# The first half of a convolution turned before the value projection, its first taps beside the indexer's chunks

## Chip, core and metric

One core of a Trainium2 chip runs the whole program in one launch. The metric is the device time of that launch in microseconds (us), the median of several executions.

## What is computed

Two layers; in each, three token mixers read the same normalised input, and one large input projection (`proj = h @ w_in`) feeds them all. Sequence 256, model width 2048, float32. Branch B holds what is moved here: a gated pair of projections, then a causal depthwise convolution of 31 taps over 1024 channels.

```
def conformer_conv(u, conv_w, conv_b, ln_w, ln_b):
    a, gt = jnp.split(u, 2, axis=-1)
    y = a * jax.nn.sigmoid(gt)
    y = lax.conv_general_dilated(y, conv_w..., window_strides=(1,), padding=[(CONV_WIDTH - 1, 0)],
                                 feature_group_count=CONV_CH) + conv_b
    y = layer_norm(y, ln_w, ln_b)
    return jax.nn.silu(y)
...
    y_a = (dsa_attention(qa, ka, va, qi, ki, wi, top_k) * jax.nn.silu(za)) @ w_a_out
    y_b = (conformer_conv(ub, ...) * jax.nn.silu(zb)) @ w_b_out
    y_c = (stick_breaking_attention(qc, kc, vc) * jax.nn.silu(zc)) @ w_c_out
    merged = g[:, :, 0] * y_a + g[:, :, 1] * y_b + g[:, :, 2] * y_c
    return x + merged @ w_out
```

## The kernel before

Every matmul multiplies float32 by splitting each operand into a high part and a low part, with three products of the parts. The weights stream from memory in units of 128x1024 numbers (512 KB). A unit goes through three engines. SyncE loads it into `raw` (five buffers). ScalarE (ACT) casts it into `wh` (L255, `high`), VectorE (DVE) subtracts into `wl` (L259, `low`), and TensorE (PE) multiplies with both. `wh` and `wl` have three buffers each, so ACT and DVE may work at most about three units ahead of PE.

The parts of a layer that matter here run in this order on PE: the opening (first half of the convolution's two gated projections, result in the two tiles `sgs`), `values(0)` (8 units, 12 matmuls of 512 columns each), `index_chunk(0)` and `index_chunk(4)` (8 units each; a unit has 6 matmuls of 512 columns and 8 of 192), then "U's group" (`run(gather(...))` with the key steps, the seven products of `Seven` for the second half of the gated projections, and the rest of that half), then `index_chunk(8)` and `(12)`. In the text, "unit 8" is the first of `index_chunk(0)`, counted from the first of `values(0)` as 0; units 8 to 23 are the two chunks, and the first key step follows them.

`turned(srcs, use)` transposes a result through memory: two STREAM_TRANSPOSE on DVE (L299), four DMAs on the POOL queue out to `z` (L302), one DMA back into `zy` (L308), and then `use`. The argument `later` says how many units after the issue `use` is placed. `use_u` copies `zy` into `yT` on ACT (L1062) and starts the taps. A tap of the convolution is done in one of two ways, chosen by the string `pace[0]` at every unit: "2" lets DVE multiply and add for two of the four channel blocks (L731), "s" lets ACT make the four products (`products_of`, L726) into a buffer, and DVE adds the buffer to the sum at a later unit (`added`, L1032). With "s" the buffer is the tile `one`, a single one; with "1" and the like it is one of two. `hold[0]` keeps the taps from being issued at all. The engines execute in the order written; Tile's scheduler writes it, so a change of the Python code moves instructions on all engines.

Of the kernel before, what the change touches and what calls it, by code (L numbers as in the profile page):

```python
# [30 lines left out]
LATER = 10  # L31
# [20 lines left out]
def trunk(ctx: ExitStack, tc: tile.TileContext, x, w_in, xt, w_a, w_b, w_c, w_out,  # L52
# [16 lines left out]
    def issue_after(ins):  # L69
        return nullcontext() if fixed[0] else tc.issue_after(ins)  # L70
# [29 lines left out]
    def nm(s):  # L100
        uid[0] += 1
        return f"{s}_{uid[0]}"
# [44 lines left out]
    def ev():  # L147
        return tp.tile([P, 512], F32, tag="ev", bufs=3, name=nm("ev"))
# [4 lines left out]
    waiting = []  # L153
# [11 lines left out]
    @contextmanager  # L165
    def in_turn():
        with tc.high_priority(offset=URGENT), issue_after(newest_parts[1].ins):
            yield
# [18 lines left out]
    def background(mm):  # L187
        while pending and pending[0][0] <= count[0]:
            step_on(pending[0])
        for e in stages[:2]:  # L190
            if e[1] <= count[0]:
                with issue_after(mm.ins), tc.high_priority() if urgent[0] else nullcontext():
                    advance(e)
                break
# [8 lines left out]
    hold, calls, pace, urgent = [False], [0], ["2"], [False]  # L203
# [59 lines left out]
    def unit(*args, **kw):  # L263
        u = load_unit(*args, **kw)
        high(u)
        low(u)
        return u[1:]
# [23 lines left out]
    def away(srcs, tmp, soon=False):  # L291

        n = len(srcs)
        k = srcs[0].shape[1]
        tmp = tmp.rearrange("p (t b k i) -> p t b k i", b=4, k=k, i=32)
        z = dp.tile([n, 4, 32, 4, k * 32], F32, tag=f"z{k}", bufs=4, name=nm("z"))
        with nullcontext() if soon else tc.high_priority():
            for t, src in enumerate(srcs):
                nc.vector.transpose(tmp[:, t].rearrange("p b k i -> p k b i"),  # L299
                                    src.rearrange("p k (b c) -> p k b c", b=4, c=32))  # L300
            for a in range(4):
                nc.gpsimd.dma_start(z[:, :, :, a, :].rearrange("t b c e -> c (t b) e"),  # L302
                                    tmp[a * 32:(a + 1) * 32].rearrange("c t b k i -> c (t b) (k i)"))
        return z

    def back(z, y):

        nc.gpsimd.dma_start(y.rearrange("p (t a) k i -> p t (a k i)", a=4), z.rearrange("t b c a e -> (b c) t (a e)"))  # L308

    def turned(srcs, use, later=LATER, tmp=None, soon=False):  # L310


        n = len(srcs)
        if tmp is None:
            tmp = tp.tile([P, n * 512], F32, tag="zt", bufs=1, name=nm("zt"))
        c = srcs[0].shape[1]
        z = away([v.rearrange("p (k e) -> p k e", e=P) for v in srcs], tmp[:, :n * c], soon)

        def rest():
            y = tp.tile([P, n * 512], F32, tag="zy", bufs=1, name=nm("zy"))  # L320
            y = y[:, :n * c].rearrange("p (u k i) -> p u k i", u=n * 4, i=32)
            back(z, y)
            yield later - 2
            yield from use(y)

        pending.append([count[0] + 2, rest()])
# [49 lines left out]
    def token_accs():  # L376
        return [acc_tile() for _ in range(NT)]
# [10 lines left out]
    def chunk_N(w, segs, act, nk, ku=2, accs=None, ks=None):  # L388
        n = sum(c for _, c in segs)
        if accs is None:  # L390
            accs = token_accs()
        for k0 in range(*(ks or (0, nk)), ku):
            background(token_products(accs, n, unit(w, k0, ku, segs), act, k0, ku, nk, range(NT)))
        return accs
# [326 lines left out]
    def products_of(yT, pr, j, q, dst, bias=False):  # L721
        for c in range(j * 4, j * 4 + 4):
            wq = pr[:, P_CW + c * TAPS + q:P_CW + c * TAPS + q + 1]
            b = dict(bias=pr[:, P_CB + c:P_CB + c + 1]) if bias else {}
            v = dst[:, c % 4 // 2, c % 2 * S:(c % 2 + 1) * S]
            nc.scalar.activation(v, yT[:, c, q:q + S], AF.Identity if bias else AF.Copy, scale=wq, **b)  # L726

    def tap(yT, cv, pr, c, q):
        wq = pr[:, P_CW + c * TAPS + q:P_CW + c * TAPS + q + 1]
        o = cv[:, c, :]  # L730
        nc.vector.scalar_tensor_tensor(o, yT[:, c, q:q + S], wq, o, op0=ALU.mult, op1=ALU.add)  # L731
# [35 lines left out]
    for layer in range(DEPTH):  # L767
# [9 lines left out]
        with tc.manual_schedule(engines={nc.vector.engine}), ExitStack() as order:  # L777
# [27 lines left out]
            sgs = [ev() for _ in range(2)]  # L805
# [217 lines left out]
        def taps(j, yT=yT, cv=cv, pr=pr, one=one, two=two, halves=halves):  # L1023

            o = cv[:, j * 4:j * 4 + 4, :]
            o2 = o.rearrange("p (t c) f -> p t (c f)", t=NT)
            state = dict(q=1, c=0, sum=None)

            def added():
                if state["sum"] is None:  # L1030
                    return False
                nc.vector.tensor_add(o2, o2, state["sum"])  # L1032
                state["sum"] = None
                return True

            halves.append(added)

            def begin():
                products_of(yT, pr, j, 0, o2, True)

            def go():
                by = pace[0][calls[0]]
                if added() and by == "s":
                    by = ""
                q = state["q"]
                if q < TAPS and by:
                    if state["c"] or by == "2":
                        for c in range(2):
                            tap(yT, cv, pr, j * 4 + state["c"] + c, q)
                        state["c"] = (state["c"] + 2) % 4  # L1050
                    else:
                        state["sum"] = one if by == "s" else two[:, q % 2]
                        products_of(yT, pr, j, q, state["sum"])
                    state["q"] += not state["c"]
                if state["q"] < TAPS or state["sum"] is not None:
                    waiting.insert(0, [0, [go]])

            waiting.append([4, [begin]])
            waiting.append([1, [go]])

        def use_u(j, y, yT=yT):
# [57 lines left out]
        def index_unit(acc, low_, k0, w_):  # L1119
            wh, wl = w_  # L1120
            for k in range(2):
                kk = k0 + k
                for i in range(2):
                    mult(acc[0], part(hx, i, kk, 1, slice(P, S))[:, 0, :], wh[:, k, :], kk + i == 0,
                         kk == KD - 1 and i == 1)
                mult(acc[1], hq[:, kk, :], wh[:, k, :], kk == 0, kk == KD - 1)
            for k in range(2):
                kk = k0 + k
                for f in range(4):
                    mm = mult(low_[:, f, :], wl[:, k, f * P:(f + 1) * P], hi(hx, kk)[:, 0, TOPK:],  # L1130
                              kk == 0 and f % 2 == 0, kk == KD - 1)
            return mm

        def low_tile():
            return mm_tile().rearrange("p (f t) -> p f t", f=4)[:, :, :S - TOPK]

        def index_done(h, acc, low_):
            e = t4()[:, :4 * (S - TOPK)].rearrange("p (k t) -> p k t", k=4)
            with tc.high_priority():
                nc.scalar.copy(e, low_)  # L1140
            turned(acc, partial(use_i, h, e), LATER + 1 if h < NIH - 4 else LATER - 2)
# [31 lines left out]
        def index_chunk(h):  # L1173
            acc, low_ = token_accs(), low_tile()
            for k0 in range(0, KD, 2):
                if (h, k0) in between:
                    between[h, k0]()
                background(index_unit(acc, low_, k0, unit(w, k0, 2, [(O_QI + h * P, 512)])))
            index_done(h, acc, low_)
# [8 lines left out]
        def values(j):  # L1188
            a = chunk_N(w, [(O_VC + j * 512, 512)], hx, KD, accs=None if j else wide_accs())
            if j:  # L1190
                with in_turn():
                    for f in halves:
                        f()
            for t in range(NT):
                with tc.high_priority():
                    nc.scalar.copy(vcr[:, t, j * 512:(j + 1) * 512], a[t])

        values(0)
        index_chunk(0)
        index_chunk(4)  # L1200
        def turn_first():
            with in_turn():
                turned(sgs, partial(use_u, 0))

        keys = key_steps()
        keys[7].at(0, turn_first)
        ring[0], spare[0] = 0, 10 ** 9
        run(gather("y*2 g.M1a y g.M5a g.M1b y g.M5b y g.M6a y g.M6b y g.M2a y g.M2b g.M7a g.M7b g.M3a c g.M3b c g.M4a d g.M4b c d c d d",
                   g=u, y=keys, c=ug, d=ua))
# [495 lines left out]
        begin = "g.M1a y g.M5a g.M1b y g.M5b y g.M6a y g.M6b y g.M2a y g.M2b y g.M7a y g.M7b "  # L1705
# [156 lines left out]
```

## Time and profile before

| | us |
|---|---|
| median of 3 runs | 1982.86 (1982.69 to 1982.94) |
| the profiled execution, its own time | 1982.91 |
| its span, first to last instruction | 1981.1 |
| PE busy | 1970.6 |
| DVE busy | 1724.0 |
| ACT busy | 1302.1 |

The share of busy time of each engine stands in the page's first section. A timeline row of the profile reads: start, duration, engine, source line, operation, tile written and tiles read, size, how many merged, and in square brackets how long the engine was idle before and what ended that. In a row of windows the brackets (x) count instructions. The lines of the source in the rows are those of the kernel before; after the change lines behind 1198 have numbers smaller by two.

### The profile page before, as it was taken

To read this page: it belongs to the slowest core of one execution; us is meant where nothing else is said; L and a number is where in the kernel's file an instruction comes from. 1 tells how busy PE (TensorE), PEld (TensorE's weight loads), DVE (VectorE), ACT (ScalarE), POOL (GpSimd) and SP (SyncE) were. 2 spreads that over 40 slices of the span, in tenths; PEclk is the share of its full clock that TensorE was granted. 3 is DMA by queue.
4 is the path that set the end of the run, shared out by engine and by line. 5 is a ranking of instruction groups with operands and counts; after the bars stand their busy time and mean duration, and the time that the engine had idled before them with its cause. 6 is when DMAs were issued, how large, how long until landed. Compare 5 with 4: busy or idle time off the path is not lost. (4 is left out here: it accounts for less than half of the span.)

```text
span 1981.1 us, 26165 instructions
## 1 busy us (share of the span) xinstructions
PE 1970.6 (99%) x9194; PEld 1648.1 (83%) x9194; DVE 1724.0 (87%) x2054; ACT 1302.1 (66%) x1668; POOL 215.0 (11%) x320
## 2 busy tenths in 40 slices
PE   9999999999999999999999999999999999999998
PEld 8888888888888888888888888888888888888886
DVE  8798999989988979878786989999888888798786
ACT  7567666579875666564565666565898766565654
POOL 0021111200200001011100210121001000010010
PEclk9999999999999999999999999999999999999999
DMA  8888768876878778787978887688669688787894
GB/s 277 278 262 261 239 180 262 257 223 188 260 239 264 212 228 271 243 273 271 321 232 277 252 264 224 192 259 273 200 188 279 213 276 250 217 276 235 288 287 137
DMA packets 247557, 486.90 MB, mean 246 GB/s; under 512 B 17984, under 2 KB 30784, under 8 KB 247296
## 3 DMA queue, kind: packets, MB, share of 16 engines
q1 hardware_dynamic: 217472, 406.03, 63.2%
q0 software_dynamic: 28288, 76.04, 14.6%
q10 hardware_dynamic: 1664, 3.15, 0.4%
q8 instruction: 72, 1.18, 0.2%
q14 instruction: 61, 0.50, 0.1%
HBM read 452.38 MB, written 32.77 MB: 245 GB/s over the span
## 5 line engine op out<-in xcount | busy, mean ns | idle before, releaser
L270 PE MATMUL acc<-wh,s 128*128 128x512 f32 x4096 | 1039.8, 390 | 0.0
L255 ACT CAST wh<-raw 128x1024 fp32r<-128x1024 f32 (+1 forms) x639 | 666.9, 1046 | 416.6 <-PE acc L270 271.2
L259 DVE TENSOR_TENSOR wl<-raw,wh 128x1024 fp32r<-128x1024 f32 (+1 forms) x640 | 773.3, 1213 | 154.7 <-ACT wh L255 147.0
L270 PEld LDWEIGHTS acc<-wh,s 128*128 128x128 f32 x4096 | 761.4, 188 | 153.2 <-DVE acc L579 0.5
L270 PE MATMUL acc<-wl,s 128*128 128x512 f32 x1856 | 517.0, 390 | 0.0
L270 PEld LDWEIGHTS acc<-wl,s 128*128 128x128 f32 x1856 | 346.0, 188 | 74.8 <-DVE wl L259 4.4
L270 PE MATMUL mm<-wh,s 128*128 128x512 f32 (+1 forms) x1376 | 335.2, 385 | 0.0
L270 PEld LDWEIGHTS mm<-wh,s 128*128 128x128 f32 x1376 | 257.3, 188 | 50.9 <-ACT ev L1688 0.5
L302 POOL DMA_DIRECT2D z<-zt x192 | 113.2, 612 | 795.6 <-DVE zt L299 743.4
L270 PE MATMUL mm<-wl,s 128*128 128x512 f32 (+1 forms) x688 | 180.9, 385 | 0.0
L255 ACT CAST wh<-ar 128x1024 fp32r<-128x1024 f32 x92 | 96.9, 1053 | 81.0 <-PE acc L270 33.6
L270 PEld LDWEIGHTS mm<-wl,s 128*128 128x128 f32 x688 | 128.7, 188 | 24.4
L259 DVE TENSOR_TENSOR wl<-ar,wh 128x1024 fp32r<-128x1024 f32 x92 | 112.1, 1220 | 21.1 <-ACT wh L255 21.1
L731 DVE SCALAR_TENSOR_TENSOR s<-yT,cst,s 128x256 f32<-128x256 f32 x216 | 94.5, 476 | 0.1
L726 ACT ACTIVATE ar<-yT,cst 128x256 f32<-128x256 f32 x192 | 83.7, 499 | 15.4 <-DVE t L1330 12.6
L255 ACT CAST wh<-va 128x1024 fp32r<-128x1024 f32 x55 | 57.7, 1050 | 44.8 <-PE acc L270 19.5
L259 DVE TENSOR_TENSOR wl<-va,wh 128x1024 fp32r<-128x1024 f32 x55 | 67.1, 1219 | 20.6 <-ACT wh L255 20.6
L528 POOL DMA_DIRECT2D ar<-in_w_in_dram x28 | 33.8, 1220 | 453.0 <-DVE wl L259 453.0
L270 PEld LDWEIGHTS mm<-s,wl 128*128 128x128 f32 x512 | 66.9, 191 | 5.0
L308 POOL DMA_DIRECT2D zy<-z x50 | 36.1, 722 | 293.2 <-DMA z<-zt 75.8
L270 PE MATMUL mm<-s,wl 128*128 128x192 f32 x512 | 66.0, 271 | 0.0
L726 ACT ACTIVATE s<-yT,cst 128x256 f32<-128x256 f32 x88 | 40.4, 517 | 38.3 <-DVE s L1032 38.1
(284 smaller groups left out, 1463.3 us busy)
## 6 DMA issues: line engine op xcount, KB each, us to landing
raw<-in_w_in_dram SPq DMA_DIRECT2D x500, 512.0 KB, 4.6
raw<-in_w_out_dram SPq DMA_DIRECT2D x50, 512.0 KB, 5.5
zy<-z POOLq DMA_DIRECT2D x48, 512.0 KB, 5.8
z<-zt POOLq DMA_DIRECT2D x184, 128.0 KB, 5.0
ar<-in_w_in_dram SPq DMA_DIRECT2D x28, 512.0 KB, 6.3
ar<-in_w_in_dram POOLq DMA_DIRECT2D x28, 512.0 KB, 9.6
raw<-in_w_b_dram SPq DMA_DIRECT2D x26, 512.0 KB, 5.1
raw<-in_w_a_dram SPq DMA_DIRECT2D x24, 512.0 KB, 6.2
```

The source lines that it names most:

```text
L255: newest_parts[0] = nc.scalar.copy(u[1], u[0])
L259: newest_parts[1] = sub = nc.vector.tensor_sub(u[2], u[0], u[1].bitcast(F32))
L270: newest[0] = nc.tensor.matmul(o, lhsT, rhs, start=start, stop=stop, skip_group_check=True)
L302: nc.gpsimd.dma_start(z[:, :, :, a, :].rearrange("t b c e -> c (t b) e"), tmp[a * 32:(a + 1) * 32].rearrange("c t b k i -> c (t b) (k i)"))
L308: nc.gpsimd.dma_start(y.rearrange("p (t a) k i -> p t (a k i)", a=4), z.rearrange("t b c a e -> (b c) t (a e)"))
L528: nc.gpsimd.dma_start((homes if own is None else third)[h], block(1, 0, h), accum_op=ALU.add)
L726: nc.scalar.activation(v, yT[:, c, q:q + S], AF.Identity if bias else AF.Copy, scale=wq, **b)
L731: nc.vector.scalar_tensor_tensor(o, yT[:, c, q:q + S], wq, o, op0=ALU.mult, op1=ALU.add)
```

## The change

Three edits. The turning of the first half (`turned(sgs, ...)`) stood at the last key step inside U's group and stands now ahead of `values(0)`, with `later` smaller by two. The taps are allowed during the two index chunks that follow, at pace "s", and then held again during U's group. The bias products of the first half (`begin`) are queued without the delay of four units.

```
@@ taps(j)
-            waiting.append([4, [begin]])
+            waiting.append([4 if j else 0, [begin]])
             waiting.append([1, [go]])
...
@@ after values() is defined
+        turned(sgs, partial(use_u, 0), LATER - 2)
         values(0)
+        hold[0], pace[0] = False, "s"
         index_chunk(0)
         index_chunk(4)
-        def turn_first():
-            with in_turn():
-                turned(sgs, partial(use_u, 0))
-
+        hold[0], pace[0] = True, "2"
         keys = key_steps()
-        keys[7].at(0, turn_first)
         ring[0], spare[0] = 0, 10 ** 9
         run(gather("y*2 g.M1a y g.M5a ...", g=u, y=keys, c=ug, d=ua))
```

The order on ACT from the end of unit 12 to the first key step, after the change (first layer; `s_82` is the buffer `one`, `yT` the turned input):

```order
L665 CAST s_8_94<-t_134_815 128x2x256
L726 ACTIVATE s_82_540<-yT_537,cst 128x256 x4
L255 CAST wh_849<-raw_847 128x1024
L726 ACTIVATE s_82_540<-yT_537,cst 128x256 x4
L255 CAST wh_873<-raw_871 128x1024
L255 CAST wh_894<-raw_892 128x1024
L726 ACTIVATE s_82_540<-yT_537,cst 128x256 x4
L255 CAST wh_931<-raw_929 128x1024
L255 CAST wh_952<-raw_950 128x1024
L726 ACTIVATE s_82_540<-yT_537,cst 128x256 x4
```

Before, only casts stood here. Now four products stand ahead of one cast and then ahead of every second, seven such blocks up to the first key step's cast.

The order on DVE over the same units, after (`s_81` is the running sum of the convolution):

```order
L259 TENSOR_TENSOR wl_850<-raw_847,wh_849 128x1024
L259 TENSOR_TENSOR wl_874<-raw_871,wh_873 128x1024
L1032 TENSOR_TENSOR s_81_539<-s_81_539,s_82_540 128x1024
L259 TENSOR_TENSOR wl_895<-raw_892,wh_894 128x1024
L259 TENSOR_TENSOR wl_932<-raw_929,wh_931 128x1024
L1032 TENSOR_TENSOR s_81_539<-s_81_539,s_82_540 128x1024
L259 TENSOR_TENSOR wl_953<-raw_950,wh_952 128x1024
```

Before, the additions were not there. Now each addition stands behind the `wl` of the unit whose cast follows the block of products on ACT, and the next block writes the buffer that this addition reads.

On ACT between `values(0)` and the chunks, where the turned data is read, after the change:

```order
L726 ACTIVATE s_82_540<-yT_537,cst 128x256 x3
L255 CAST wh_772<-raw_770 128x1024
L1196 COPY s_82_540<-mm_558 128x512 x2
L726 ACTIVATE s_81_539<-yT_537,cst 128x256
L255 CAST wh_793<-raw_791 128x1024
L726 ACTIVATE s_81_539<-yT_537,cst 128x256 x3
L665 CAST s_7_93<-t_127_759 128x2x256
L665 CAST s_8_94<-t_127_759 128x2x256
L665 CAST s_7_93<-t_134_815 128x2x256
L255 CAST wh_828<-raw_826 128x1024
```

Ahead of these rows stand the copy into `yT` (right behind the cast of unit 8), one product and the cast of unit 9; the casts here are those of units 10, 11 and 12. Before, the copy and the products were not in this stretch.

## Rows read from the trace of the kernel before

**Rows 1.** The page, section 1: busy us, share, instructions.

```profile
PE 1970.6 (99%) x9194; PEld 1648.1 (83%) x9194; DVE 1724.0 (87%) x2054; ACT 1302.1 (66%) x1668; POOL 215.0 (11%) x320
```

**Rows 2.** All waits of PE: total us, times, longest.

```profile
PE mm L1431 <- DVE s L1546: 1.1, 1, 1.1
PE mm L916 <- DVE eps L79: 1.1, 1, 1.1
```

**Rows 3.** Windows: index chunks, U's group, the end of the program.

```profile
71.04:107.27 36.23, 36.23 (x225) 32.29 (x224) 23.58 (x23) 19.90 (x24) 3.22 (x5) 1.00 0.91 306
107.27:157.60 50.33, 50.33 (x242) 44.30 (x241) 49.27 (x60) 34.30 (x42) 10.94 (x16) 1.00 0.83 254
...
1960.00:1981.00 21.00, 12.74 (x62) 10.59 (x61) 12.96 (x34) 6.40 (x15) 0.00 (x0) 0.93 0.26 101
```

**Rows 4.** Timeline of PE: unit 8, first key step, low products of M1b.

```profile
71.04 1.52 PE L270 MATMUL acc<-wh,s 128*128 128x512 f32 x6
...
107.27 1.62 PE L270 MATMUL mm<-wh,s 128*128 128x400 f32 x8
...
118.05 0.73 PE L270 MATMUL acc<-wl,s 128*128 128x512 f32 x2
```

**Rows 5.** Timeline of ACT: cast of unit 8, evictions, casts of 512.

```profile
64.89 1.05 ACT L255 CAST wh<-raw 128x1024 fp32r<-128x1024 f32 x1 [1.66 <-PE mm L270]
...
71.29 1.07 ACT L1196 COPY s<-mm 128x512 f32<-128x512 f32 x2
...
73.72 1.66 ACT L665 CAST s<-t 128x512 fp32r<-128x512 f32 x3
```

**Rows 6.** Timeline of ACT: the copy into yT, a block of products, casts.

```profile
157.92 1.05 ACT L1062 COPY yT<-zy 128x1024 f32<-128x1024 f32 x1
...
280.11 1.71 ACT L726 ACTIVATE s<-yT,cst 128x256 f32<-128x256 f32 x4 [4.50 <-DVE s L1032]
281.73 2.93 ACT L255 CAST wh<-raw 128x1024 fp32r<-128x1024 f32 x3
```

**Rows 7.** Timeline of DVE, and last the additions L1032 (ns min/median/max).

```profile
52.42 1.22 DVE L259 TENSOR_TENSOR wl<-raw,wh 128x1024 fp32r<-128x1024 f32 x1 [0.23 <-ACT wh L255]
...
103.00 0.99 DVE L259 TENSOR_TENSOR wl<-raw,wh 128x800 fp32r<-128x800 f32 x1 [0.89 <-ACT wh L255]
...
106.17 1.22 DVE L511 TENSOR_TENSOR ph<-ph,ar 128x1024 f32<-128x1024 f32 x1
...
112.23 1.23 DVE L259 TENSOR_TENSOR wl<-ar,wh 128x1024 fp32r<-128x1024 f32 x1 [0.47 <-ACT wh L255]
...
116.78 1.22 DVE L259 TENSOR_TENSOR wl<-raw,wh 128x1024 fp32r<-128x1024 f32 x1
...
L1032 DVE TENSOR_TENSOR s<-s,s x18: 1206/1218/1227, 227.2 to 1376.4; 128x1024 f32<-128x1024 f32 x18
```

**Rows 8.** One turning (DVE, POOL), then zy's issue to landing in us.

```profile
136.49 0.70 DVE L299 STREAM_TRANSPOSE zt<-ev 128x512 f32<-128x512 f32 x1
...
137.50 2.37 POOL L302 DMA_DIRECT2D z<-zt  x4 [8.99 <-DVE zt L299]
145.54 0.73 POOL L308 DMA_DIRECT2D zy<-z  x1 [5.67 <-DVE t L1084]
...
zy<-z POOLq DMA_DIRECT2D x48, 512.0 KB, 5.8
...
DMA to landing us min/median/max: 4.5/6.2/10.1
```

**Rows 9.** Second layer: DVE in the values stage, PE at unit 8.

```profile
1035.55 1.23 DVE L259 TENSOR_TENSOR wl<-raw,wh 128x1024 fp32r<-128x1024 f32 x1
1036.68 1.29 DVE L792 TENSOR_TENSOR s<-s,s 128x512 fp32r<-128x512 f32 x2
...
1053.84 1.52 PE L270 MATMUL acc<-wh,s 128*128 128x512 f32 x6
```

**Rows 10.** Window in the stick-breaking stage of the first layer.

```profile
440.00:480.00 40.00, 40.00 (x178) 32.77 (x178) 35.66 (x37) 39.92 (x67) 0.00 (x0) 1.00 0.58 171
```

## Prediction

> **What bounds the kernel now.** I read the page's busy times first, then the waits of PE, then the stretch of the change in windows and timelines. PE is busy for 1970.6 of 1981.1 us [rows 1], so 10.5 us are idle. The wait view of PE has two lines only: 1.1 us at the very start and 1.1 us in the second layer [rows 2]; the last window adds 21.00 - 12.74 = 8.3 us behind the last matmul [rows 3]. Between the opening and the end PE stands still once, for 1.1 us. Nothing that makes DVE, ACT, POOL or a DMA cheaper can give back more than that 1.1 us, 0.06%. A measurement of this kernel tells about 0.2%, 4.0 us, from no change. What the change can do is take away slack, so the question is how much slack the casts and subtractions have where work is put in. In the two index chunks ACT is busy for 19.9 and DVE for 23.6 of 36.2 us; in U's group DVE is busy for 49.3 of 50.3 us [rows 3]. The first place looks roomy, and the second is full. It lives on slack that it brings along: the `wl` of M1b is ready at 116.78 + 1.22 = 118.00 [rows 7], and PE wants it at 118.05 [rows 4].
>
> **The change, part by part.** Removed from U's group: two transpositions on DVE (0.70 each [rows 8]) and five DMA issues on POOL. DVE stays ahead of PE there in the trace, so this is worth nothing by itself; it comes behind M1b, too late for what follows. Added to the values stage: the same two transpositions. Their subtractions and low parts still come ahead of PE (a delay of about 1.2 us against slack of some 2 to 4), so nothing. The removed delay of `begin` only lets the first products start earlier. What then follows is fewer taps later, where PE waits for nothing: nothing again. The four DMAs to `z` and the one back find the POOL queue empty.
>
> The cost lies on ACT, in three steps, counted against PE's unchanged times. (1) **The copy into `yT` waits for a transfer, and the casts queue behind it.** DVE's `wl` at 52.42 had 0.23 us of idle time before it [rows 7]; with one transposition ahead of it and one behind, and 0.08 overlap at three seams (1035.55 + 1.23 against 1036.68 [rows 9]), the second ends at 52.42 - 0.23 + 0.70 + 1.22 + 0.70 - 0.24 = 54.6. POOL follows 0.3 later (136.49 + 0.70 against 137.50), the issue back 8.0 after that (145.54), and the data lands 5.8 us later in the median, 4.5 to 10.1 at the extremes [rows 8]: 54.6 + 0.3 + 8.0 + 5.8 = 68.7. ACT is at the copy at 64.89 + 1.05 = 65.9 [rows 5] and stands for 2.8 us. Queued behind it are the casts of units 9 to 12, for which PE waits.
>
> The row of the way back is weighed here against a rule. The Trainium skill (DMA: Bandwidth & Descriptors, "Anatomy of one DMA — SWDGE (gpsimd) path") puts a DMA at about 2.0 us plus its bytes at 436 GB/s. That gives an estimate of 2.3 us for 128 KB and 3.2 us for 512 KB; the data would land near 62, ACT would not wait, and the total below would be 7 us, not 13. The rows, 8.0 and 5.8 us for the two legs, say nearly twice that, and they decide.
>
> From 68.7 ACT has, up to the first block of products that waits for an addition: the copy 1.05, eight products at 1.62 / 4 = 0.405 (280.11 to 281.73), four casts at 0.94 (three take 2.93, one 1.05) [rows 6], two evictions 0.97 and four casts of 512 at 0.52 (1.07 and 1.66 less 0.1 of overlap [rows 5]). That is 1.05 + 3.24 + 3.76 + 0.97 + 2.08 = 11.1, so the block starts at 79.8. The block after it needs the next addition, behind which DVE has one `wl` and two low parts: 1.22 + 1.22 and, as an estimate, twice 0.62 as for a transposition, less overlap, 3.4 us. It starts at 83.2.
>
> (2) **A ring of ACT and DVE that is longer than PE's two units.** From here the order is products, cast, cast on ACT and `wl`, addition, `wl` on DVE. The products of a block overwrite the only buffer, so they wait for the addition; the addition stands behind the `wl` of the next unit; that waits for its cast, which stands behind the previous block. One turn takes 1.62 (products) + 1.05 (cast) [rows 5, 6] + 1.22 (`wl`) + 1.22 (addition) [rows 7] = 5.1 us. PE does two units in 2 x (107.27 - 71.04) / 16 = 4.53 us [rows 4]. Each turn loses 0.6 us although both engines have idle time. Five turns follow: 83.2 + 25.5 = 108.7 for the last block. Behind it stands the cast for the first key step: 108.7 + 1.62 + 0.86 (800 of 1024 columns, an estimate from 1.05) = 111.2. PE wants it at 107.27, so PE is late by 3.9 us here.
>
> (3) **U's group no longer has the slack that it used up.** DVE does two `wl` of 0.99 less overlap, 1.8, and then the chain from L511 to the `wl` of M1b, which in the trace takes 116.78 + 1.22 - 106.17 - 0.47 idle = 11.4 us [rows 7]: 111.2 + 1.8 + 11.4 = 124.4, wanted at 118.05. PE is late by 6.3 us; behind that point DVE has two transpositions less and keeps up. These are not added to the 3.9: the last lateness contains the earlier ones. First layer: **+6.3 us**.
>
> Second layer: the second transposition ends at 1036.68 + 2 x 0.70 - 0.08 = 1038.0 [rows 9], the data lands at 1052.1. Unit 8 begins at 1053.84, 982.80 later than in the first layer, so this is 69.3 on the first layer's clock, 0.6 later; the order is the same. **+6.9 us**. Sum: 13.2. The profiled execution took 1982.91, within 0.05 of the median: 1982.9 + 13.2 = **1996.1**. The 1.1 us wait of the second layer is left in, since no tap stands near it; if it goes, 1995.0.
>
> Bounds of the unknown: with 4.5 us of landing each layer loses 1.3 less, 13.2 - 2.6 = 10.6, and without the old wait 9.5; with 10.1 us each loses 4.3 more, 21.8.
>
> **Rivals.** *The data is early.* If `zy` landed before 65.9, ACT would not stand, and the whole chain would start 2.8 (first layer) and 3.4 us (second) earlier: 3.5 + 3.5 = 7.0, 1989.9. The ring and U's group remain. Against it: 8.0 + 4.5 from the rows is already 67.4.
>
> *No loss.* ACT can be full without PE waiting: from 440 to 480 it is busy for 39.9 of 40 us, with products between the casts, and PE does not wait [rows 10]. If the products fit into the idle time of ACT and DVE in the chunks in this way, lateness stays below the slack of about 5 us at unit 8 (cast ended 65.9, wanted 71.04) and U's group catches up: 1982.9. It decides if a turn of the ring is at most 4.53 us. For it: the idle time, 16 us of ACT [rows 3]. Against it: in that stretch the products alternate between two buffers, and a unit of PE is longer; here the buffer is single, and a block waits for DVE in the trace for up to 4.50 us [rows 6]. The Trainium skill (Perfetto Trace Analysis, "Optimizing Scalar/DVE Operations") also advises giving work of a saturated DVE to ScalarE, which would speak for the change; the trace agrees that DVE is saturated in U's group, but the products are run elsewhere.
>
> *Faster.* The wait at L1546 goes and nothing is lost: 1981.8, which counts as no change. More than 4 us of gain has no place in the trace.
>
> **How the numbers follow.** The loss as told: 0.70, 1992.4 to 2004.7. Early data: 0.12. No loss: 0.10, with the 1.1 us gain in it. A transfer still later or loads that come late because `raw` is freed late, beyond 2004: 0.06. Faster by over 0.2%: 0.02. So slower 0.88, same 0.10, faster 0.02. The range leaves out no loss and the late end: 1989.0 to 2003.0.
>
> **What would show it.** In the changed profile PE waits for `wh` L255 some five times by about 0.6 us between 80 and 112 us, each two units apart, and twice by over 1 us for `wl` L259 near 118 and 124; the same again about 983 us later. ACT's waits at L726 for L1032 grow by some seven a layer. PE's busy time stays near 1971 and its idle time grows from 10.5 to about 24. ACT stands ahead of the copy into `yT` for about 3 us, ended by `zy`. I am wrong if PE shows no waits in the chunks, if the copy starts near 66, or if U's group keeps up although it starts late.

## The result, and the profile of the changed kernel

| | before | after |
|---|---|---|
| median, us | 1982.78 (1982.64 to 1982.94, 4 runs) | 1995.32 (1994.87 to 1997.40, 4 runs) |
| ratio, 95% interval | 1 | 1.0065 (1.0048 to 1.0083) |
| span of the profiled execution | 1981.1 | 1993.3 |
| PE busy | 1970.6 | 1974.8 |
| PE idle (span less busy) | 10.5 | 18.5 |

The change makes the kernel 12.5 us slower; 13.2 were forecast. The page of the changed kernel, section 1, answers to [rows 1]:

```profile
PE 1974.8 (99%) x9194; PEld 1649.5 (83%) x9194; DVE 1723.0 (86%) x2066; ACT 1289.9 (65%) x1648; POOL 215.4 (11%) x320
```

ACT and DVE are even a little less busy than before, so neither has more work to do. All waits of PE after the change (us in total, times, longest) answer to [rows 2]:

```profile
PE acc L270 <- ACT wh L255: 4.1, 13, 0.4
PE acc L270 <- DVE wl L259: 3.6, 4, 1.0
PE mm L916 <- DVE eps L79: 1.1, 1, 1.1
PE mm L270 <- DVE wl L259: 0.9, 3, 0.4
```

Twenty waits for weights are new. The wait of 1.1 us in the second layer for L1546 is gone. The windows of the two index chunks and of U's group, at the times of [rows 3] (span, then busy time of PE, PE's weight loads, DVE, ACT and POOL, granted clock, DMA share, GB/s):

```profile
71.04:107.27 36.23, 33.80 (x198) 28.73 (x197) 27.02 (x28) 29.95 (x53) 3.05 (x5) 1.00 0.76 252
107.27:157.60 50.33, 48.37 (x238) 42.40 (x237) 48.36 (x55) 34.65 (x45) 8.60 (x12) 1.00 0.82 246
```

The granted clock is 1.00 in both, as before, so the loss is not one of the clock. In the chunks PE is no longer full although ACT has 6 and DVE 9 us to spare. The timeline of PE after the change, first layer, shows where; three more waits of 0.34 follow at 96.67, 101.81 and 106.94, each two units behind the last:

```profile
82.00 1.14 PE L270 MATMUL mm<-s,wl 128*128 128x192 f32 x8 [0.38 <-DVE wl L259]
...
86.41 1.66 PE L270 MATMUL acc<-wh,s 128*128 128x512 f32 x6 [0.41 <-ACT wh L255]
...
88.78 1.56 PE L270 MATMUL acc<-wh,s 128*128 128x512 f32 x6
90.17 1.03 PE L270 MATMUL mm<-s,wl 128*128 128x192 f32 x8
91.54 1.66 PE L270 MATMUL acc<-wh,s 128*128 128x512 f32 x6 [0.34 <-ACT wh L255]
...
111.89 1.72 PE L270 MATMUL mm<-wh,s 128*128 128x400 f32 x8
...
118.42 0.73 PE L270 MATMUL acc<-wl,s 128*128 128x512 f32 x2 [1.01 <-DVE wl L259]
...
125.00 0.73 PE L270 MATMUL acc<-wl,s 128*128 128x512 f32 x2 [0.81 <-DVE wl L259]
```

The first key step, at 107.27 before [rows 4], starts at 111.89: 4.6 us late. The low products of M1b, at 118.05 before, start at 125.00: 6.95 us late. The loss of the first layer is complete there. The same places in the second layer, after the change:

```profile
1061.51 1.52 PE L270 MATMUL acc<-wh,s 128*128 128x512 f32 x6
...
1114.83 0.74 PE L270 MATMUL acc<-wl,s 128*128 128x512 f32 x2 [0.80 <-DVE wl L259]
```

And the low products there before:

```profile
1100.85 0.73 PE L270 MATMUL acc<-wl,s 128*128 128x512 f32 x2
```

PE comes late to unit 8 by 1061.51 - 1053.84 [rows 9] = 7.7 us, and the low products start 14.0 late, so that layer adds 6.3. The span ends 12.2 later: some 1.8 come back behind that point, most of it at the wait that is gone.

The timeline of ACT after the change, first layer:

```profile
64.88 1.05 ACT L255 CAST wh<-raw 128x1024 fp32r<-128x1024 f32 x1 [1.15 <-PE mm L270]
68.66 1.05 ACT L1062 COPY yT<-zy 128x1024 f32<-128x1024 f32 x1 [2.72 <-DMA zy<-z]
...
80.24 1.71 ACT L726 ACTIVATE s<-yT,cst 128x256 f32<-128x256 f32 x4
81.86 1.03 ACT L255 CAST wh<-raw 128x1024 fp32r<-128x1024 f32 x1
83.71 1.71 ACT L726 ACTIVATE s<-yT,cst 128x256 f32<-128x256 f32 x4 [0.82 <-DVE s L1032]
...
88.84 1.71 ACT L726 ACTIVATE s<-yT,cst 128x256 f32<-128x256 f32 x4 [1.54 <-DVE s L1032]
90.46 1.98 ACT L255 CAST wh<-raw 128x1024 fp32r<-128x1024 f32 x2
93.98 1.71 ACT L726 ACTIVATE s<-yT,cst 128x256 f32<-128x256 f32 x4 [1.54 <-DVE s L1032]
...
109.38 1.71 ACT L726 ACTIVATE s<-yT,cst 128x256 f32<-128x256 f32 x4 [1.53 <-DVE s L1032]
110.99 2.56 ACT L255 CAST wh<-raw 128x800 fp32r<-128x800 f32 x3
```

And of DVE, one turn of the ring:

```profile
86.39 1.23 DVE L259 TENSOR_TENSOR wl<-raw,wh 128x1024 fp32r<-128x1024 f32 x1 [1.58 <-ACT wh L255]
87.53 1.22 DVE L1032 TENSOR_TENSOR s<-s,s 128x1024 f32<-128x1024 f32 x1
88.67 1.22 DVE L259 TENSOR_TENSOR wl<-raw,wh 128x1024 fp32r<-128x1024 f32 x1
91.52 1.23 DVE L259 TENSOR_TENSOR wl<-raw,wh 128x1024 fp32r<-128x1024 f32 x1 [1.64 <-ACT wh L255]
```

The reader can walk round the ring in these rows. ACT's block ends at 85.4, its first cast behind that ends at 86.4, DVE's `wl` starts at 86.39 after 1.58 us of idle time, the addition at 87.53, and ACT's next block, idle for 1.54 us until then, at 88.84. From 83.71 to 109.38 five turns take 25.67 us, 5.13 each. ACT waits in every turn, DVE waits in every turn, and PE, which needs two units in 4.53, waits too.

### The profile page after: what moved, and what is told of

Same layout as the page of the kernel before. It is cut to its first block, busy times and chain, and to the rows that moved or that the text cites. A ratio compares the mean times of both kernels' runs of the same rounds, so it can differ in the third digit from the quotient of the medians.

```text
span 1993.3 us, 26150 instructions
## 1 busy us (share of the span) xinstructions
PE 1974.8 (99%) x9194; PEld 1649.5 (83%) x9194; DVE 1723.0 (86%) x2066; ACT 1289.9 (65%) x1648; POOL 215.4 (11%) x320
## 4 chain that ended last, share of the span: by engine, by line
PE 91%; DVE 3%; ACT 3%; issue 2%; DMA 1%; POOL 0%; DVEq 0%; ACTq 0%; POOLq 0%
PE acc L270 65%; PE mm L270 23%; ACT s L726 1%; DVE s L1032 1%; ACT wh L255 1%; DVE wl L259 1%; PE mm L1263 1%; DMA z<-zt 0%; PE mm L1353 0%; PE mm L1452 0%; PE mm L1321 0%; PE mm L1399 0%; DMA zy<-z 0%; PE mm L1429 0%; PE mm L916 0%
## 5 line engine op out<-in xcount | busy, mean ns | idle before, releaser
L726 ACT ACTIVATE s<-yT,cst 128x256 f32<-128x256 f32 x152 | 67.4, 509 | 56.4 <-DVE s L1032 56.2
L731 DVE SCALAR_TENSOR_TENSOR s<-yT,cst,s 128x256 f32<-128x256 f32 x232 | 100.6, 473 | 0.0
L308 POOL DMA_DIRECT2D zy<-z x50 | 36.2, 723 | 278.8 <-DMA z<-zt 94.5
L726 ACT ACTIVATE ar<-yT,cst 128x256 f32<-128x256 f32 x112 | 49.3, 504 | 19.1 <-DVE t L1328 8.5
```

## The experiments

The runs of before beside these spread more than in the first measurement (1981.8 to 1984.6 over 63 runs), so a single profiled execution can stand 1 to 2 us from its median, and differences of about 2 us are read by the intervals.

A trace is one execution, and it can already be 0.7 us late where the stretch of the change begins. So the loss of a layer is read inside each trace. From the start of unit 8 to the start of the low products of M1b the kernel before takes 47.01 us in either layer (71.04 to 118.05, 1053.84 to 1100.85). What the other kernels take more, by the starts of the same two matmul groups:

| us more than 47.01 | first layer | second layer |
|---|---|---|
| the changed kernel | 7.0 | 6.3 |
| the turning alone | 0.8 | 0.0 |
| a second buffer | 0.4 | 1.9 |
| the copy later | 5.8 | 5.6 |
| taps in the second chunk alone | 1.8 | 1.4 |
| taps in the first chunk alone | 3.5 | 2.2 |
| taps in one layer alone | 6.6 | 0.0 |
| both mends | 0.0 | 0.0 |
| the taps on DVE | 1.1 | 2.0 |
| the taps on DVE and the copy later | 0.0 | 1.3 |

**The turning alone.** Nothing is left out; the taps come later instead.

```
         values(0)
-        hold[0], pace[0] = False, "s"
+        pace[0] = "2"
         index_chunk(0)
         index_chunk(4)
```

> The first half is still turned ahead of the value projection, but no tap is issued in the two index chunks. Theory of the ring: the copy into yT still waits some 2.7 us for its data, as in the changed kernel, but ACT has 16 us of idle time in the chunks (36.2 less 19.9 busy before) and no products to wait for, so it catches up before U's group: PE waits nowhere between 71 and 158 us, 1982.9, or 1981.7 if the wait at L1546 in the second layer is gone too. Rival, the transfer is the cause (all casts are late because the copy stands for 2.7 us ahead of them): PE is late by up to the 1.8 us that the changed kernel has lost at unit 14, twice, 1986.5. Rival, the turning costs by itself ahead of the values: waits of PE before unit 8.

Measured: 1981.68 us, ratio 0.9996 (0.9987 to 1.0005). ACT stands 3.07 us at the copy, longer than in the changed kernel, and by the wait view PE waits nowhere in the chunks; only 0.2 us at one `wl` of U's group and 0.7 at 190 us are left, and the wait at L1546 is gone here too. By the starts the first layer still loses 0.8 us: about half behind casts that waited for weight loads (ACT idle for up to 3.00 us until `raw` came), the rest at that `wl`. Whether the turning delays these loads is not shown. One block of four products still stands behind the copy, put there by the scheduler, and then only casts and evictions up to the first key step. Turning early and waiting for the transfer cost at most these 0.8 us and, in the second layer, nothing, as long as no ring follows. The two rivals of this run fall.

**A second buffer.** The half `cv[:, 4:8]` of the convolution's sum, unused until U's group is done, takes every second block.

```
+        other = cv[:, 4:8, :].rearrange("p (t c) f -> p t (c f)", t=NT)
...
-                        state["sum"] = one if by == "s" else two[:, q % 2]
-                        products_of(yT, pr, j, q, state["sum"])
+                        state["sum"] = (one if q % 2 else other) if by == "b" else one if by == "s" else two[:, q % 2]
+                        with issue_after(newest_parts[0].ins) if by == "b" else nullcontext():
+                            products_of(yT, pr, j, q, state["sum"])
...
-        hold[0], pace[0] = False, "s"
+        hold[0], pace[0] = False, "b"
```

> The changed kernel with every second block of products written into a second buffer (the half of cv that is not yet in use), and held behind the same cast on ACT, so that the blocks from unit 13 on, the casts and the additions stand in the order of the changed kernel; the amount of work is the same. Theory of the ring: a block no longer waits for the addition before it. Two units then cost ACT 1.62 + 2 x 0.95 = 3.5 us against 4.53 of PE, so the five losses of 0.6 us per layer go. What stays is the entry, 0.7 to 1.8 us a layer up to unit 14, and some of the 2.3 us in U's group: 1984.3 to 1989, with 1985.5 as the single figure. PE has no waits between units 16 and 23. Rival, too much work: ACT and DVE cannot do casts, products and additions in the time whatever the buffers, 1993 or more, with the waits at units 16 to 23 as they are. Rival, U's group alone (it loses 2.3 us a layer because of what is moved out of or into its neighbourhood): the 2.3 stays in full.

Measured: 1985.26 us, ratio 1.0015 (1.0006 to 1.0024): 10 of the 12.5 us are gone with no less work; the order of the blocks and casts from unit 13 on stays, and one block more stands ahead of the first key cast. Timeline of ACT:

```profile
82.13 1.71 ACT L726 ACTIVATE s<-yT,cst 128x256 f32<-128x256 f32 x4
83.74 1.99 ACT L255 CAST wh<-raw 128x1024 fp32r<-128x1024 f32 x2
85.63 1.71 ACT L726 ACTIVATE s<-yT,cst 128x256 f32<-128x256 f32 x4
87.24 2.00 ACT L255 CAST wh<-raw 128x1024 fp32r<-128x1024 f32 x2
89.13 1.72 ACT L726 ACTIVATE s<-yT,cst 128x256 f32<-128x256 f32 x4
```

Window of the two chunks, same kernel:

```profile
71.04:107.27 36.23, 36.23 (x221) 31.95 (x220) 30.98 (x33) 34.31 (x61) 3.05 (x5) 1.00 0.86 290
```

The same three instructions now take 3.5 us (85.63 - 82.13) with no wait between them. In the window ACT and DVE are each some 4 us busier than in the changed kernel, where they stood still for each other, and PE is full. So the loss in the chunks is not one of too much work: the wait for the addition makes it. U's group, whose casts are in time again, loses 0.16 us by the idle column in the first layer and nothing in the second. What is left in the stretch stands at the entry of the second layer: two waits of 0.33 and 0.47 us, 1.9 us by the starts, behind a copy for which ACT waited 3.39 us.

**The copy one cast later.**

```
-        turned(sgs, partial(use_u, 0), LATER - 2)
+        turned(sgs, partial(use_u, 0), LATER)
```

> The changed kernel with the copy into yT placed two units later than in it, so that it stands behind the cast of unit 9 and the data should have landed when ACT comes to it. Theory of the ring: the wait at the copy goes, and with it up to 1.8 us a layer, but the slack that it had eaten is eaten by the ring (six turns of 5.13 against 4.53 us) and U's group still loses 2.3: 4.5 to 6.0 us a layer, 1991 to 1994. Rival, the transfer is the cause: 1983.

Measured: 1995.05 us, ratio 1.0062 (1.0049 to 1.0075), a microsecond above what was expected. Timeline of ACT:

```profile
68.01 1.06 ACT L255 CAST wh<-raw 128x1024 fp32r<-128x1024 f32 x1 [1.66 <-PE mm L270]
69.15 1.05 ACT L1062 COPY yT<-zy 128x1024 f32<-128x1024 f32 x1
...
82.91 1.71 ACT L726 ACTIVATE s<-yT,cst 128x256 f32<-128x256 f32 x4 [2.17 <-DVE s L1032]
```

Timeline of PE, the two ends of the stretch in the first layer:

```profile
71.44 1.52 PE L270 MATMUL acc<-wh,s 128*128 128x512 f32 x6
...
124.21 0.74 PE L270 MATMUL acc<-wl,s 128*128 128x512 f32 x2 [0.81 <-DVE wl L259]
```

The copy no longer waits, and the two waits at the entry are gone. But the ring still forms, 0.8 us earlier (82.91 against 83.71), and PE loses 124.21 - 71.44 - 47.01 = 5.8 us in the first layer and 5.6 in the second, within the 4.5 to 6.0 expected, where the changed kernel loses 7.0 and 6.3. The transfer is not the main cause: by the traces the wait at the copy is worth 1.9 us of 13.3. The medians cannot show so little (this interval alone is 5 us wide). The run does not test earlier data, since the copy itself stands 0.5 us later.

**Taps in the second chunk alone.**

```
-        hold[0], pace[0] = False, "s"
         index_chunk(0)
+        hold[0], pace[0] = False, "s"
         index_chunk(4)
```

> Taps are allowed only in the second of the two index chunks, from unit 16 on; the copy is where it is in the changed kernel. Theory of the ring: ACT recovers from the copy in the first chunk; four turns at a loss of 0.6 us then only eat slack, so PE loses little in the chunk (0 to 1 us), but the first casts of U's group come late and PE loses there 2.3 us a layer as in the changed kernel: 1982.9 + 2 x (2.3 to 3.3) = 1987.5 to 1989.5, less 1.1 if the wait at L1546 goes. Rival, loss in proportion to the products issued: 4 of 7 blocks, 4 of 6.95 us a layer, spread over the chunk, 1990.8. Rival, U's group is only slow because PE had already waited in the chunks: no waits there, 1983 to 1985.

Measured: 1986.87 us, ratio 1.0019 (1.0011 to 1.0028). Timeline of PE from the first key step on:

```profile
107.39 1.62 PE L270 MATMUL mm<-wh,s 128*128 128x400 f32 x8
...
113.40 0.74 PE L270 MATMUL acc<-wl,s 128*128 128x512 f32 x2 [0.58 <-DVE wl L259]
...
119.98 0.73 PE L270 MATMUL acc<-wl,s 128*128 128x512 f32 x2 [0.82 <-DVE wl L259]
```

PE waits nowhere in the chunks and starts U's group on time (107.39 against 107.27). Yet it loses 1.8 us in U's group (1.4 in the second layer), a place where no tap is issued: the ring had used up the slack of the casts, and the saturated DVE there cannot give it back.

**Taps in the first chunk alone.**

```
         index_chunk(0)
+        hold[0] = True
         index_chunk(4)
```

> Taps are allowed only in the first of the two index chunks (units 8 to 15) and held from unit 16 on. Theory of the ring: PE loses what the changed kernel has lost when it comes to unit 16 or 17, 2.4 us a layer or up to 0.6 less; with no products in the second chunk ACT and DVE regain some 2 us for every two units and U's group starts in time and loses at most 0.3: 1982.9 + 2 x (1.8 to 2.7) = 1986.5 to 1988.3, less 1.1 where the wait at L1546 goes. Rival, U's group loses 2.3 us a layer whatever comes before: 1991.

Measured: 1988.06 us, ratio 1.0032 (1.0020 to 1.0045). Here it is the other way round: PE waits five times from 80.95 to 92.72 us, and from there to 121.71, the start of the low products of M1b, it waits no more. Eight units without products are enough for U's group to lose nothing. The first layer loses 3.5 us, more than the 1.8 to 2.7 expected; and as the wait at L1546 is gone, the time is a microsecond above what was expected.

**Taps in one layer alone.**

```
-        hold[0], pace[0] = False, "s"
+        hold[0], pace[0] = layer > 0, "s"
```

> The changed kernel with the taps in the chunks of the first layer alone; in the second layer the half is only turned early, as in the run with the turning alone. Theory of the ring: the first layer loses its 6.9 us as before and the second nothing: 1982.7 + 6.9 = 1989.6, less 1.1 if the wait at L1546 in the second layer goes with the turning alone (as its time of 1981.7 suggests): 1988.5. Rival, the wait at L1546 only goes because the second layer's taps come early: 1989.6 with that wait in the trace.

Measured: 1989.75 us, ratio 1.0036 (1.0023 to 1.0049), the profiled execution 1988.38. The low products of M1b start at 124.69, 6.64 us late, there are no waits between 1040 and 1120 us, and none at L1546: the two layers lose separately, and the old wait goes with the early turning alone. By the median of five runs (1988.38 to 1992.34) the rival's number is nearer; by the trace its wait is not there.

**Both mends.** The second buffer and the later copy together.

> Both mends of the changed kernel at once: the second buffer of the run with two buffers, and the copy into yT two units later. Alone the later copy gave nothing worth naming (1995.05 against 1995.3) and the second buffer gave 10 of 12.5 us. Theory of the ring: with the ring gone the slack of some 5 us at unit 8 is no longer eaten, so the entry that the later copy spares stays spared: PE waits nowhere in the chunks and at most 0.2 us a layer in U's group, 1981.5 to 1983. Rival, the two causes just add: the second buffer's result less the 0.25 us that the later copy gave alone, 1985.0.

Measured: 1983.33 us, ratio 1.0005 (0.9997 to 1.0014), 1.9 us below the second buffer alone. PE has no wait in the chunks or in U's group, and by the starts the stretch loses nothing in either layer. This does not speak against the rival that the two causes add: by the traces the later copy is worth 1.9 us in the changed kernel and 2.3 here; only the medians, 0.3 and 1.9, look different. The number missed its bound by 0.3 us: six waits of 0.15 to 0.30 us stand at 267 to 293 and 1251 to 1277 us, in a later stage. What order makes them was not followed up.

**The taps on DVE.** DVE does two channel blocks of a tap at every unit, ACT none.

```
-        hold[0], pace[0] = False, "s"
+        hold[0], pace[0] = False, "2"
```

> The changed kernel with the taps of the two chunks done by DVE alone (two channel blocks of one tap at every unit, 0.47 us each by the rows of L731), no products on ACT: about as many taps, and no buffer between the two engines. DVE was busy for 23.6 of 36.2 us there; 16 units with 0.95 us make it 38.8, more than the window, less overlap some 37. Theory of the ring: the ring cannot form; DVE is just full, so PE waits for wl rather than wh and loses 1 to 3 us a layer, some at the entry and some in U's group: 1984 to 1988.5. Rival, too much work: the loss is set by what the fuller of the two engines lacks, and here DVE lacks more than ACT did, so it is no better than the changed kernel, 1995.

Measured: 1982.51 us, ratio 1.0000 (0.9991 to 1.0009), better than expected. Windows of the chunks and of U's group:

```profile
71.04:107.27 36.23, 35.66 (x217) 31.06 (x216) 34.73 (x55) 22.96 (x31) 3.04 (x5) 1.00 0.82 281
107.27:157.60 50.33, 50.33 (x246) 44.43 (x245) 49.70 (x59) 34.99 (x43) 8.58 (x12) 1.00 0.83 246
```

Its two waits of PE for weights:

```profile
82.53 1.14 PE L270 MATMUL mm<-s,wl 128*128 128x192 f32 x8 [0.57 <-DVE wl L259]
...
1066.43 1.14 PE L270 MATMUL mm<-s,wl 128*128 128x192 f32 x8 [1.14 <-DVE wl L259]
```

Timeline of DVE, same kernel:

```profile
87.64 1.23 DVE L259 TENSOR_TENSOR wl<-raw,wh 128x1024 fp32r<-128x1024 f32 x1
88.77 0.88 DVE L731 SCALAR_TENSOR_TENSOR s<-yT,cst,s 128x256 f32<-128x256 f32 x2
89.56 1.23 DVE L259 TENSOR_TENSOR wl<-raw,wh 128x1024 fp32r<-128x1024 f32 x1
```

DVE is busy for 34.73 of 36.23 us and holds PE up only once per layer, at the entry (0.57 and 1.14 us by the idle column, 1.1 and 2.0 by the starts). One unit costs DVE 89.56 - 87.64 = 1.92 us against PE's 2.26; the expectation allowed too little for overlaps and so took DVE for overfull. The 1.1 and 2.0 lie in the 1 to 3 us a layer that it forecast; the time is that of before because as much comes back outside the stretch, 1.3 us of it at L1546, whose wait is gone here too. Behind the entry DVE, at 96%, works without a break and PE waits nowhere; two engines at 83% and 75% that wait for each other cost 6 to 7 us a layer.

**The taps on DVE and the copy later.** The edits of the last run and of the later copy.

> The run with the taps on DVE, and the copy into yT placed two units later, behind the cast of unit 9. In the run with the taps on DVE PE lost time only at the entry: waits of 0.57 and 1.14 us in the idle column, and by the starts of the same matmuls some 1.1 and 1.8 us in the two layers. Theory of the ring: without the wait at the copy these go too, and since nothing else is full, 1982.5 - 2.9 = 1979.6, or up to 0.5 us a layer more where U's group, which now gets its first subtractions later, loses some: 1979.5 to 1981.5. Rival, the entry costs because of the work put in there (copy, products and evictions in a row) and not because of the wait: no change, 1982.5.

Measured: 1980.51 us, ratio 0.9990 (0.9981 to 0.9999) over 11 runs. PE has one wait of 0.71 us left at the entry of the second layer and none in U's group. In the first layer the copy does not wait and the stretch loses nothing; in the second ACT still stood 2.26 us until the data came, and PE lost 1.3. (The profiled execution, 1982.54, is one of the two slowest of the 11.) This is the only one of nine versions whose interval against before lies below 1, and only just, so the gain of 2 us is not certain.

## Why the prediction was right

The forecast was 1996.1 within 1989 to 2003, slower with a chance of 0.88; the median is 1995.32.

*What bounds the kernel* held in the main: the change took slack. But the statement that nothing cheaper on another engine can give back more than 1.1 us is too strong: it leaves out the 8.3 us behind the last matmul, which are idle time of PE too, and the wait at L1546 alone gave back 1.3 us by the starts.

*Step 1, the copy waits.* Forecast for the first layer: the data at 68.7. Measured: the copy starts at 68.66 after a wait of 2.72 us. POOL's rows of the changed kernel show the first leg:

```profile
54.84 2.47 POOL L302 DMA_DIRECT2D z<-zt  x4 [54.39 <-DVE zt L299]
62.85 0.73 POOL L308 DMA_DIRECT2D zy<-z  x1 [5.54 <-DMA z<-zt]
```

The legs took 8.0 us (62.85 - 54.84) and 5.8 us (68.66 - 62.85), as [rows 8] had it. For the first leg this is partly luck: in the row that the forecast took, the profile has the issue back waiting for DVE (L1084), not for the four transfers. A turning of the kernel before that did wait for them agrees, with 97.86 - 90.05 = 7.8 us:

```profile
90.05 2.49 POOL L302 DMA_DIRECT2D z<-zt  x4 [89.60 <-DVE zt L299]
97.86 0.73 POOL L308 DMA_DIRECT2D zy<-z  x1 [5.32 <-DMA z<-zt]
```

The rule of the Trainium skill (DMA: Bandwidth & Descriptors, "Anatomy of one DMA — SWDGE (gpsimd) path") gives estimates of 2.3 and 3.2 us for transfers of these sizes, and this trace does not agree: from issue to landing they took 4.4 and 5.4 us in the median of the changed kernel's page. How much of that is due to the weight loads beside them (DMA share 0.88 from 53 to 69 us) no run separates. The forecast's bounds for the landing, 4.5 to 10.1 us, are those of the transfers from 100 to 300 us; over the whole trace of before they are 3.9 to 10.4.

What step 1 did not say, and the runs show, is what the wait is worth by itself. Where the copy was moved behind a further cast, the stretch lost 1.9 us less over both layers with the ring, 2.3 less with the second buffer and 1.8 less with the taps on DVE, by the starts; the medians of the last two pairs agree (1985.26 to 1983.33, 1982.51 to 1980.51). Without taps behind it the wait costs at most 0.8 us (the turning alone). So it adds about 2 us, and the ring and what it does to U's group the other 11. In the second layer the data was forecast 0.6 later against unit 8 than in the first; it came 0.5 earlier, since the way back took 4.9 us. ACT waited only 2.21 us there, and the layer lost 6.3 where 6.9 stood. The rival of early data, 7.0 us, was not tried.

*Step 2, the ring.* Forecast: the first waiting blocks at 79.8 and 83.2, a turn of 5.1, the last block at 108.7, the cast of the first key step at 111.2. Measured: 80.24, 83.71, 5.13, 109.38, and with one cast of 0.86 us 110.99 + 0.86 = 111.85; PE comes to the first key step 4.6 us late, where 3.9 stood. The second buffer shows the cause: the order stays and the work is no less, but the waits go. ACT's waits at L726 for L1032 grew from 16 to 28, six a layer (seven were forecast).

*Step 3, U's group.* Forecast: 6.3 us late at the `wl` of M1b; measured 6.95, of which 0.65 was there with the first key cast (111.85 against 111.2). Taps in the second chunk alone show it by itself: on time at the start of the group, 1.8 us late after it. Taps in the first chunk show its condition: with eight units free of products ahead of it, the group loses nothing.

*The size* came out right partly by offsets, which is luck. The layers lost 6.95 and 6.3, together 13.25 against 13.2. Not forecast were 0.7 us more between the two layers, where waits of 0.28 and 0.15 us are new at 296.76 and 299.97. Left in the sum was the wait at L1546, which went; the text had named that as 1995.0. That it goes with the early turning alone is shown (the turning alone, taps in one layer alone); by which order on DVE was not followed up.

*One sign was read wrongly.* PE's busy time was to stay near 1971 and its idle time to grow to about 24; they are 1974.8 and 18.5. The waits in the chunks were to be about 0.6 us each and the two in U's group over 1; they are 0.29 to 0.41, 1.01 and 0.81. A turn loses 5.13 - 4.53 = 0.60 us, but its row shows an idle time of 0.34. The rest is in the busy time, in a profile that models the ends of matmuls: at 90.17 a group of matmuls starts 0.17 before the one ahead of it has its modelled end (88.78 + 1.56), and at a wait this overlap is lost; and the first group behind a wait takes 1.66 instead of 1.56.

*The rivals.* "No loss" named its point: a turn of at most 4.53 us. What stood against it was stronger than said: before the change a block waits for DVE for up to 5.8 us, not 4.50. With two buffers the same three instructions take ACT 3.5 us, PE waits nowhere in the chunks of the first layer, and in the second at the entry alone. The Trainium skill's advice that spoke for it (Perfetto Trace Analysis, "Optimizing Scalar/DVE Operations": some work of a saturated DVE may go to ScalarE) has no ground in this stretch: in the chunks DVE was not saturated (23.6 of 36.2 us [rows 3]), and with the taps on it instead of on ACT the kernel is 12.8 us faster than the change.

## What to carry to other kernels

Before work is put into the idle time of two in-order engines, follow one item round: if A waits for B's last result, and B's result stands behind work that waits for A, the length of that ring counts and not the busy shares; compare it with the time that the bounding engine gives, here 5.13 against 4.53 us. A second buffer, or the work on one engine alone, opens the ring. Slack that is eaten in a roomy stretch is paid in the next full one, so look for the loss there too.

## What the runs showed of the hardware

A short wait of PE costs more than its idle column says: 0.34 us shown, 0.60 us lost by the starts (5.13 against 4.53 for two units). In the rows the overlap of neighbouring matmul groups (0.17) goes, and the first group behind the wait is 0.10 longer; as the ends of matmuls in the profile are modelled, only the starts, and so the 0.60, are measured. The loss per wait is read from the starts of the same matmul in two traces.
